# A transformer block's w_down in seven products: the sums of its weights from accumulating DMAs, and another order of the products

## The chip, the core and the metric

The kernel runs on one core of a Trainium2 chip. The metric is the device time of one execution in microseconds, as the median of several executions. The engines of the core work side by side, each through its own queue in program order: TensorE (PE, with its weight loads as PEld), VectorE (DVE), ScalarE (ACT), GpSimd (POOL) and SyncE (SP), which here issues nearly all DMAs.

## What is computed

One block of a decoder on 512 tokens of width 1024, in float32: two token mixers, then an MLP, then a gated per-layer embedding. The change touches the MLP and the passage to the last part:

```python
h2 = rms_norm(x, norm_mlp[i])
x = x + jnp.square(jax.nn.relu(h2 @ w_up[i])) @ w_down[i]        # 1024 -> 4096 -> 1024

ple_gate = jax.nn.sigmoid(rms_norm(x, norm_ple[i]) @ w_ple_gate[i])
x = x + ple_gate * (p[i] @ w_ple[i])
```

## The kernel before

Every float32 product is made of three matmuls (`mm3`, lines 100 to 104): an operand is split into an upper half (an ACT copy, rounded) and a lower half (DVE, the difference; `halves`, lines 161 to 164), and upper times upper, upper times lower and lower times upper are added up in PSUM. So each weight tile of 512 KB that comes in by DMA costs a 128x1024 copy on ACT and a 128x1024 subtraction on DVE. The halves rotate through three buffers each (`whi`, `wlo`), so that a tile can be split once the tile three before it is used up. The raw tiles have three buffers too (`raw`).

The order of the work is written out by hand. A *tick* is a point in the program after each half block, 12 matmuls of 128x128 by 128x512; a block (one output tile of w_up, or one product below) is two half blocks. `at(t, f)` puts work on tick t, and `spawn` starts a generator that goes on by a step at each tick (a `yield n` waits n ticks); what is emitted at a tick stands on each engine's queue at that place. Engines and DMA queues are bound to the order within their own queue and by the semaphores of the data, not to ticks as such.

The MLP starts at tick T0 = 178 and goes through the hidden layer in four quarters of 1024 hidden units, 30 ticks each. A quarter has eight tiles of w_up (U0 to U7; `unit` loads each seven ticks ahead of its use and `make` starts its split three ticks ahead), whose ReLU-squared outputs stand in `F`. Then w_down's quarter is multiplied by seven products in place of eight, after Strassen and Winograd: with activations A and weights split in two by two parts (A11, A12, A21, A22 below are the weights' parts, two tiles each), products are made of sums of parts, and their results are added to `acc` in several places. The diff names them P1 to P7; they run as P5, P1, P6, P2, P7, P3, P4, and U0 to U3 of the next quarter are put between the last four (`up_ahead`).

Two kinds of sums are needed. The weights' sums are made by GpSimd (`add`, line 282, eight for each quarter): A21 + A22 for P5, plus A11 for P6, plus A12 for P3, in a slot v; A21 + A11 for P7. The activations' sums (lines 879 to 888): each tile of U0 to U3 gives its part of the difference for P5, on GpSimd; each of U4 to U7 changes the first half of F in place, on GpSimd for U4 to U6 and on DVE for U7, one tick after its square. From these the operands are split into `ta` and `tb` (`later`, lines 910 to 917): P5 and P1 use ta, P6 and P2 use tb, P7 and P3 ta again, P4 tb. P6 reads the finished sum of the first half, P2 the second half as it came out of w_up, P1 the first half as it was before U4.

After the last quarter, `turn_back` transposes `acc` by TensorE back to the layout of x, adds it to x1 (which came back from DRAM as `x2`), splits the result scaled by the norm's gain, and adds up its squares; two of its four calls stand within and behind the last product, P4, at the ticks TP - 2 and TP - 1 (TP = T0 + 120 is where the embedding starts), the other two between the first matmuls of w_ple. The last call spawns `norm_end`, which sums over the partitions by a matmul (lines 364 and 365) and leads to R2. `load_p` loads the embedding's input p and splits it.

Of the kernel before, what the change touches and what calls it, by code (L numbers as in the profile page):

```python
# [21 lines left out]
F32 = mybir.dt.float32  # L22
# [24 lines left out]
def kernel(ctx: ExitStack, tc: tile.TileContext, xT, pT, w_in, w_val, w_glr, w2, cols,  # L47
# [213 lines left out]
    def make(raw):  # L261
# [2 lines left out]
        ready.append((hi, lo))  # L264
        jobs.insert(0, [halves(hi, lo, raw), 0])

    def down_units(g):

        d0 = T0 + 30 * g + 16
        gap = 2 if g < 3 else 0  # L270
        box = {}

        def load(t, name, tag, src):
            def f():
                if name not in box:
                    box[name] = [slot(f"{tag[0]}{int(tag[1:]) + j}", [P, 2, 512]) for j in range(2)] \
                        if tag[0] == "v" else slot(tag, [P, 2, 2, 512])
                nc.sync.dma_start(out=box[name][:, t % 2], in_=src)
            return f

        def add(out, a, b):
            G.tensor_tensor(out(), a(), b(), ALU.add)  # L282

        for u in range(2):
            a11, a12 = w_down[0, 4 * g + u], w_down[0, 4 * g + 2 + u]
            a21, a22 = w_down[1, 4 * g + u], w_down[1, 4 * g + 2 + u]

            def W(name, u=u):
                return lambda: box[name][:, u]

            def S(u=u):
                if u not in sums:
                    sums[u] = slot(f"v{u}", [P, 2, 512])
                return sums[u]
# [11 lines left out]
            at(d0 + u + 3, lambda W=W: make(W("A12")()))  # L306
            at(d0 + u + 4, load(u, "A22b", "c1", a22))
            at(d0 + u + 4, lambda S=S, W=W: add(S, S, W("A12")))
            at(d0 + u + gap + 5, lambda W=W: make(W("A21")()))
            at(d0 + u + 2 * gap + 7, lambda S=S: make(S()))  # L310
            at(d0 + u + 3 * gap + 9, lambda W=W: make(W("A22b")()))

    sums = {}
    for g in range(4):
        for j in range(8):
            c = T0 + 30 * g + 2 * j
            unit(c if g == 0 or j > 3 else c - 6 + 2 * j, w_up[8 * g + j, 0])
        at(T0 + 30 * g + 8, sums.clear)
        down_units(g)
    TP = T0 + 120  # L320
    unit(TP, w_ple[0])
    for j in range(8):
        unit(TP + 2 + 2 * j, w_gate[j, 0])
# [532 lines left out]
    def half_of(t):  # L856
        return t.rearrange("p (t c) -> p t c", t=2)

    ffs = {}

    def ahead_of(g):

        F = slot("a0", [P, 2, KT, 256])
        box = []

        def up_evac(i, ps):
            e = F[:, :, i]
# [5 lines left out]
            def rest():  # L873
                if not g and not i:
                    yield 2
                    V.tensor_tensor(e, e, half_of(R1), ALU.mult)
                A.activation(e, e, AF.Square)  # L877
                yield 1
                k = i % 4
                if i < 4:  # L880
                    if not box:
                        box.append(slot("c2", [P, 4, 256]))
                    G.tensor_tensor(box[0][:, k], F[:, 0, i], F[:, 1, i], ALU.subtract)  # L883
# [5 lines left out]
            spawn(rest())  # L889

        ffs[g] = F, up_evac, box
        return up_evac

    ahead_of(0)

    def up_down(g):
        nonlocal acc
        u0 = T0 + 30 * g
        d0 = u0 + 16
        F, up_evac, box = ffs.pop(g)  # L900
        ta = slot("a1", [P, 2, 2, 4, 256], F32R)
        tb = slot("a2", [P, 2, 2, 4, 256], F32R)

        def t_split(t, i, src):
            yield from halves(t[:, i, 0], t[:, i, 1], src)

        def later(t, gen):
            at(t, lambda: spawn(gen))
# [5 lines left out]
        later(d0 + 4, t_split(ta, 0, F[:, 1, :4]))  # L914
        at(d0 + 4, lambda: G.tensor_tensor(F[:, 0, 4:], F[:, 0, 4:], F[:, 0, :4], ALU.subtract))
        later(d0 + 6, t_split(ta, 1, F[:, 1, 4:]))
        later(d0 + 8, t_split(tb, 0, F[:, 0, 4:]))

        gemm_fm(8 if g == 0 else 4, kt_of(h2_hi, h2_lo), lambda i, ps: up_evac(i + (4 if g else 0), ps))

        if acc is None:
            acc = slot("a6", [P, NT, D])

        def part(n, t, m):
            return acc[:, 2 * t + m, n * T:(n + 1) * T]

        def product(t, i):
            ps = [bank(), bank()]
            for u in range(2):
                w = ready.pop(0)  # L930
                for k in range(2):
                    for m in range(2):
                        ms = slice(m * P, (m + 1) * P)
                        mm3(ps[m], (t[:, i, 0, 2 * u + k, ms], t[:, i, 1, 2 * u + k, ms]),
                            (w[0][:, k], w[1][:, k]), u == 0 and k == 0, u == 1 and k == 1)
                if u == 0:
                    tick()
            return ps

        new = g == 0  # L940
        ahead = ahead_of(g + 1) if g < 3 else None

        def up_ahead(i):
            if ahead:
                gemm_fm(1, kt_of(h2_hi, h2_lo), lambda _, ps: ahead(i, ps))

        for m, ps in enumerate(product(ta, 0)):
            subtotal(new, part(0, 1, m), ps, ALU.add)
            subtotal(new, part(1, 1, m), ps, ALU.subtract)
        tick()  # L950
        y = [tt("y"), tt("y")]
        for m, ps in enumerate(product(ta, 1)):
            A.activation(y[m], ps, AF.Copy)
            subtotal(new, part(0, 0, m), ps, ALU.add)
        tick()
        for m, ps in enumerate(product(tb, 0)):
            V.tensor_tensor(y[m], ps, y[m], ALU.subtract)
            G.tensor_tensor(part(0, 1, m), part(0, 1, m), y[m], ALU.subtract)
        tick()
        for m, ps in enumerate(product(tb, 1)):  # L960
            subtotal(False, part(0, 0, m), ps, ALU.add)
        tick()
        up_ahead(0)
        for m, ps in enumerate(product(ta, 0)):
            V.tensor_tensor(y[m], ps, y[m], ALU.add)
            G.tensor_tensor(part(1, 1, m), part(1, 1, m), y[m], ALU.add)
            if new:
                G.tensor_scalar(part(1, 0, m), y[m], 1.0, 1.0, ALU.mult, ALU.mult)
            else:
                G.tensor_tensor(part(1, 0, m), part(1, 0, m), y[m], ALU.add)  # L970
        tick()
        up_ahead(1)
        for m, ps in enumerate(product(ta, 1)):
            subtotal(False, part(0, 1, m), ps, ALU.add)
        tick()
        if g == 3:
            at(d0 + 12, lambda: turn_back(0))
            at(d0 + 13, lambda: turn_back(2))
        up_ahead(2)
        for m, ps in enumerate(product(tb, 0)):  # L980
            subtotal(False, part(1, 0, m), ps, ALU.add)
        tick()
        up_ahead(3)

    def turn_back(i0):

        nonlocal s2, R2
        for i in range(i0, i0 + 2):
# [34 lines left out]
    for g in range(4):  # L1023
        up_down(g)


    mid = slot("a1", [P, KT, T])
# [132 lines left out]
```

## Time and profile before

| | us |
|---|---|
| median of 3 runs | 1000.03 |
| lowest and highest | 999.83, 1000.47 |
| the profiled execution | 999.96 |
| its span, from the first to the last instruction | 998.2 |
| around the span | 1.8 |

| engine | busy us | share of the span |
|---|---|---|
| PE (matmul) | 965.1 | 97% |
| PEld (weight load, beside PE) | 799.5 | 80% |
| DVE | 634.9 | 64% |
| ACT | 471.0 | 47% |
| POOL (GpSimd) | 302.9 | 30% |

The MLP lies between about 565 and 918 us of the span. Times in the rows are microseconds from the span's start, unless marked ns. A timeline row gives start, duration, engine, line, operation and the tiles written and read, with the idle time in front of it and who ended it in brackets. A matmul's duration is longer than its distance from the next one, since matmuls overlap; their pace is read from the starts. PEclk is the granted clock of TensorE as a share of full speed, so that 1.00 is 2.4 GHz and 0.50 is 1.2 GHz.

### The profile page before, as it was taken

To read this page: it belongs to the slowest core of one execution; us is meant where nothing else is said; L and a number is where in the kernel's file an instruction comes from. 1 tells how busy PE (TensorE), PEld (TensorE's weight loads), DVE (VectorE), ACT (ScalarE), POOL (GpSimd) and SP (SyncE) were. 2 spreads that over 40 slices of the span, in tenths; PEclk is the share of its full clock that TensorE was granted. 3 is DMA by queue.
4 is the path that set the end of the run, shared out by engine and by line. 5 is a ranking of instruction groups with operands and counts; after the bars stand their busy time and mean duration, and the time that the engine had idled before them with its cause. 6 is when DMAs were issued, how large, how long until landed. Compare 5 with 4: busy or idle time off the path is not lost.

```text
span 998.2 us, 11425 instructions
## 1 busy us (share of the span) xinstructions
PE 965.1 (97%) x4360; PEld 799.5 (80%) x4360; DVE 634.9 (64%) x807; ACT 471.0 (47%) x691; POOL 302.9 (30%) x200
## 2 busy tenths in 40 slices
PE   9999999999999999999999998999899999989698
PEld 7888888878888888888888887888688778867586
DVE  5468889785456843333555557755874776589564
ACT  5558879773237632122323445423533433344551
POOL 0027656411220000000000038427652934665300
PEclk9999999999999999999999999999899989989799
DMA  7222111113211223343233443115214311551041
GB/s 254 85 84 85 64 57 64 64 64 106 85 61 45 88 103 105 106 169 106 85 105 127 148 169 133 57 59 193 85 64 169 122 68 43 190 190 42 22 148 42
DMA packets 29430, 101.22 MB, mean 101 GB/s; under 512 B 3392, under 2 KB 3776, under 8 KB 28992
## 3 DMA queue, kind: packets, MB, share of 16 engines
q1 hardware_dynamic: 29232, 100.48, 28.7%
q8 instruction: 34, 0.56, 0.2%
q14 instruction: 20, 0.16, 0.1%
q10 hardware_dynamic: 144, 0.02, 0.0%
HBM read 96.29 MB, written 4.19 MB: 101 GB/s over the span
## 4 chain that ended last, share of the span: by engine, by line
PE 88%; DVE 8%; ACT 2%; issue 1%; POOLq 0%; POOL 0%; ACTq 0%; DVEq 0%
PE acc L102 22%; PE acc L103 22%; PE acc L104 22%; PE aux L104 6%; PE aux L103 6%; PE aux L102 6%; DVE wlo L164 3%; DVE a L164 2%; DVE a L850 1%; PE aux L562 1%; ACT whi L162 1%; PE aux L729 1%; PE aux L365 1%; PE aux L364 1%; PE aux L732 1%
## 5 line engine op out<-in xcount | busy, mean ns | idle before, releaser
L102 PE MATMUL acc<-a,whi 128*128 128x512 f32 x832 | 326.4, 392 | 0.0
L103 PE MATMUL acc<-a,whi 128*128 128x512 f32 x832 | 324.3, 390 | 0.0
L104 PE MATMUL acc<-a,wlo 128*128 128x512 f32 x832 | 324.1, 390 | 0.0
L164 DVE TENSOR_TENSOR wlo<-raw,whi 128x1024 fp32r<-128x1024 f32 x128 | 167.7, 1313 | 79.3 <-ACT whi L162 77.9
L104 PEld LDWEIGHTS acc<-a,wlo 128*128 128x128 f32 x832 | 156.3, 188 | 32.9
L102 PEld LDWEIGHTS acc<-a,whi 128*128 128x128 f32 x832 | 156.6, 188 | 32.2
L103 PEld LDWEIGHTS acc<-a,whi 128*128 128x128 f32 x832 | 156.5, 188 | 31.8
L162 ACT ACTIVATE whi<-raw 128x1024 fp32r<-128x1024 f32 x128 | 134.2, 1049 | 86.6 <-PE acc L103 73.3
L104 PE MATMUL aux<-whi,a 128*128 128x512 f32 x288 | 116.9, 406 | 14.9 <-DVE a L164 14.9
L883 POOL TENSOR_TENSOR c<-a 128x256 f32<-128x256 f32 x16 | 13.8, 863 | 340.3 <-ACT a L877 340.3
L102 PE MATMUL aux<-whi,a 128*128 128x512 f32 x288 | 116.8, 406 | 0.0
L103 PE MATMUL aux<-wlo,a 128*128 128x512 f32 x288 | 115.9, 402 | 0.0
L104 PEld LDWEIGHTS aux<-whi,a 128*128 128x128 f32 x288 | 56.6, 197 | 28.6 <-DVE a L164 16.6
L164 DVE TENSOR_TENSOR wlo<-c,whi 128x1024 fp32r<-128x1024 f32 x32 | 53.0, 1672 | 22.9 <-ACT whi L162 22.9
L102 PEld LDWEIGHTS aux<-whi,a 128*128 128x128 f32 x288 | 56.7, 197 | 12.7 <-ACT a L162 0.8
L103 PEld LDWEIGHTS aux<-wlo,a 128*128 128x128 f32 x288 | 56.7, 197 | 12.5 <-DVE wlo L164 0.4
L162 ACT ACTIVATE whi<-c 128x1024 fp32r<-128x1024 f32 x32 | 33.9, 1060 | 60.7 <-PE aux L104 39.7
L877 ACT ACTIVATE a<-a 128x512 f32<-128x512 f32 x32 | 20.0, 627 | 68.2 <-DVE a L869 64.8
L492 POOL TENSOR_TENSOR ql<-q,qh 128x512 fp32r<-128x512 f32 x16 | 22.3, 1392 | 87.1 <-ACT qh L490 87.1
L282 POOL TENSOR_TENSOR v<-v,c 128x1024 f32<-128x1024 f32 x16 | 45.8, 2861 | 8.3 <-DVE wlo L164 8.3
L164 DVE TENSOR_TENSOR a<-a,a 128x1024 fp32r<-128x1024 f32 x24 | 43.3, 1804 | 6.6 <-ACT a L162 6.6
L164 DVE TENSOR_TENSOR wlo<-v,whi 128x1024 fp32r<-128x1024 f32 x24 | 41.2, 1742 | 7.6 <-ACT whi L162 7.6
(211 smaller groups left out, 1387.7 us busy)
## 6 DMA issues: line engine op xcount, KB each, us to landing
raw<-in_w_in_dram SPq DMA_DIRECT2D x48, 512.0 KB, 3.2
c<-in_w_down_dram SPq DMA_DIRECT2D x40, 512.0 KB, 5.5
raw<-in_w_up_dram SPq DMA_DIRECT2D x32, 512.0 KB, 3.4
raw<-in_w_val_dram SPq DMA_DIRECT2D x14, 512.0 KB, 3.3
raw<-in_w_a_dram SPq DMA_DIRECT2D x8, 512.0 KB, 3.3
raw<-in_w_b_dram SPq DMA_DIRECT2D x8, 512.0 KB, 3.3
raw<-in_w_out_dram SPq DMA_DIRECT2D x8, 512.0 KB, 3.3
raw<-in_w_gate_dram SPq DMA_DIRECT2D x8, 512.0 KB, 3.3
```

What stands on the lines that cost most here:

```text
L102: PE.matmul(ps, a[0], b[0], start=start, stop=False)
L103: PE.matmul(ps, a[0], b[1], start=False, stop=False)
L104: PE.matmul(ps, a[1], b[0], start=False, stop=stop)
L162: A.activation(hi, src, AF.Copy)
L164: (eng or V).tensor_tensor(lo, src, f32(hi), ALU.subtract)
L282: G.tensor_tensor(out(), a(), b(), ALU.add)
L364: PE.matmul(ps, ones[n], sh, start=True, stop=False)
L365: PE.matmul(ps, ones[n], sl, start=False, stop=True)
L492: G.tensor_tensor(sl, q2, f32(sh), ALU.subtract)
L562: PE.transpose(ps[:, c + (i - b) * P:c + (i - b + 1) * P], p[:, i, b * P:(b + 1) * P], ident)
L877: A.activation(e, e, AF.Square)
L883: G.tensor_tensor(box[0][:, k], F[:, 0, i], F[:, 1, i], ALU.subtract)
```

## The change

The weights' sums are no longer added by GpSimd from two tiles in SBUF. The first part is loaded into the sum's tile, and each further part is added to it by a DMA that GpSimd issues with `accum_op=ALU.add`, which reads the part from DRAM and adds it to what stands in the tile. In the last quarter the sum for P3 is made anew in two raw tiles by a load and three such DMAs each (`last_sum`), rather than carried on from P6's.

The order of the blocks becomes U4 U5 U6 P5 U7 P1 P2 P6 U0' P7 U1' P3 U2' P4 U3' in each quarter (the primes are the next quarter's tiles), so that P5 stands ahead of U7, and P2 ahead of P6. The loads, sums and splits take their ticks from the blocks' starts. For U7, square, differences and the split for P2 are emitted together in its evacuation; the other tiles keep their tick between the square and the differences. `norm_end` of x2 starts a tick later, and the load and the split of p move towards TP: the load from tick TP - 11 to TP - 4, the split from about TP - 5 to TP - 3.

```diff
+    blocks = [("U", 0, j) for j in range(4)]
+    for g in range(4):
+        mix = ["U4", "U5", "U6", "P5", "U7", "P1", "P2", "P6", "n0", "P7", "n1", "P3", "n2", "P4", "n3"]
+        for z in mix:
+            k = int(z[1])
+            if z[0] != "n":
+                blocks.append((z[0], g, k))
+            elif g < 3:
+                blocks.append(("U", g + 1, k))
+    start = {z: T0 + 2 * j for j, z in enumerate(blocks)}
+    TP = T0 + 2 * len(blocks)
+
     def down_units(g):
...
+        c = {k: start["P", g, k] for k in range(1, 8)}
...
-        def add(out, a, b):
-            G.tensor_tensor(out(), a(), b(), ALU.add)
...
+        def add(t, name, u, src):
+            at(t, lambda: G.dma_start(out=of(name, u), in_=src, accum_op=ALU.add))
+
+        def use(k, name, u):
+            at(c[k] + u - 3, lambda: make(of(name, u)))
...
-            at(d0 + u - 8, load(u, "A21", "c0", a21))
-            at(d0 + u - 8, load(u, "A22", "c3", a22))
-            at(d0 + u - 5, load(u, "A11", "c1", a11))
-            at(d0 + u - 5, lambda S=S, W=W: add(S, W("A21"), W("A22")))
-            at(d0 + u - 3, lambda S=S: make(S()))
-            at(d0 + u - 1, lambda S=S, W=W: add(S, S, W("A11")))
-            at(d0 + u - 1, lambda W=W: make(W("A11")()))
-            at(d0 + u - 1, load(u, "A12", "c3", a12))
-            at(d0 + u + 1, lambda S=S: make(S()))
-            at(d0 + u + 2, lambda W=W: add(W("A21"), W("A21"), W("A11")))
...
-            at(d0 + u + 4, lambda S=S, W=W: add(S, S, W("A12")))
...
+            t = c[5] + u
+            S = f"S{u}"
+            load(t - 10, S, f"v{u}", u, a22)
+            load(t - 9, "A21", "c0", u, a21)
+            load(t - 8, "A11", "c1", u, a11)
+            load(t - 1, "A12", "c3", u, a12)
+            load(c[1] + u, "A22", "c1", u, a22)
+            add(t - 8, S, u, a21)
+            add(t - 5, "A21", u, a11)
+            add(t - 1, S, u, a11)
+            if g < 3:
+                add(c[6] + u - 1, S, u, a12)
+            else:
+                last_sum(t, u, (a22, a21, a11, a12))
+            for k, name in ((5, S), (1, "A11"), (6, S), (2, "A12"), (7, "A21"), (3, S), (4, "A22")):
+                if g < 3 or k != 3:
+                    use(k, name, u)
+                else:
+                    at(c[3] + u - 3, lambda u=u: make(sums[u]))
...
+    def last_sum(t, u, srcs):
+
+        def f():
+            sums[u] = wp.tile([P, 2, 512], F32, tag="raw", name=nm("raw"))
+            nc.sync.dma_start(out=sums[u], in_=srcs[0])
+        at(start["U", 3, 7] + u - 6, f)
+        for j in range(3):
+            at(start["U", 3, 7] + u + 3 * j - 4, lambda j=j: G.dma_start(out=sums[u], in_=srcs[j + 1],
+                                                                     accum_op=ALU.add))
...
+    def quarter(g):
...
+        e7 = start["U", g, 7] + 1
...
+        c5 = start["P", g, 5]
+        at(c5 - 6, begin)
+        later(c5 - 4, lambda: t_split(ta, 0, t1))
+        later(c5 - 5, lambda: t_split(ta, 1, F[:, 0, :4]))
+        later(e7 + 1, lambda: t_split(tb, 0, F[:, 0, :4]))
+        later(e7 + 3, lambda: t_split(ta, 0, F[:, 1, :4]))
+        at(e7 + 4, t4_sum)
+        later(e7 + 5, lambda: t_split(ta, 1, F[:, 1, 4:]))
+        later(start["P", g, 6] + 2, lambda: t_split(tb, 0, F[:, 0, 4:]))
...
-        later(d0 - 6, t_split(ta, 1, F[:, 0, :4]))
-        at(d0 - 5, lambda: spawn(t_split(ta, 0, box[0])))
-        later(d0 + 2, t_split(tb, 0, F[:, 0, :4]))
-        later(d0 + 3, t_split(tb, 1, F[:, 0, 4:]))
...
-                yield 1
+                if i < 7:
+                    yield 1
+                pieces()
...
+            if i < 7:
+                spawn(squares())
+            else:
+                for _ in squares():
+                    pass
+                for _ in t_split(tb, 1, F[:, 0, 4:]):
+                    pass
...
-                spawn(norm_end(R2, s2))
+                spawn(norm_end(R2, s2), 1)
...
-        yield 6
+        yield 1
         p_hl = slot("c0", [P, 4, T], F32R)
...
-    at(T0 + 106 + 1, back_x1)
-    at(T0 + 106 + 3, lambda: spawn(load_p()))
+    at(start["P", 3, 1] + 1, back_x1)
+    at(start["P", 3, 3], lambda: spawn(load_p()))
+    at(TP - 2, lambda: turn_back(0))
+    at(TP - 1, lambda: turn_back(2))
```

## Rows read from the trace of the kernel before

**Rows 1.** the page's first part: busy us (share) xinstructions

```profile
PE 965.1 (97%) x4360; PEld 799.5 (80%) x4360; DVE 634.9 (64%) x807; ACT 471.0 (47%) x691; POOL 302.9 (30%) x200
```

**Rows 2.** who TensorE waited for, whole span: total us, times, longest

```profile
PE aux L104 <- DVE a L164: 14.9, 4, 3.7
PE acc L102 <- ACT a L1052: 6.3, 2, 3.7
...
PE aux L991 <- DVE a L850: 2.2, 2, 1.9
PE aux L364 <- ACT qh L92: 2.0, 1, 2.0
```

**Rows 3.** timeline, TensorE, first quarter: start us, us, instruction [idle]

```profile
609.11 0.39 PE L104 MATMUL acc<-a,wlo 128*128 128x512 f32 x1
609.33 0.39 PE L102 MATMUL aux<-whi,a 128*128 128x512 f32 x1
...
620.44 0.39 PE L103 MATMUL aux<-wlo,a 128*128 128x512 f32 x1
624.51 0.67 PE L104 MATMUL aux<-whi,a 128*128 128x512 f32 x1 [3.69 <-DVE a L164]
...
628.26 0.39 PE L104 MATMUL aux<-whi,a 128*128 128x512 f32 x1
```

**Rows 4.** stretches: length, PE, PEld, DVE, ACT, POOL busy (x), PEclk, DMA

```profile
620.43:628.25 7.82, 4.13 (x11) 2.97 (x10) 6.30 (x4) 3.40 (x6) 4.32 (x2) 0.78 0.57 225
707.39:717.01 9.62, 5.89 (x15) 4.34 (x15) 7.89 (x7) 3.29 (x5) 4.84 (x2) 0.65 0.49 195
795.46:805.62 10.16, 6.43 (x16) 4.76 (x16) 7.89 (x6) 3.83 (x6) 5.39 (x2) 0.66 0.46 179
883.85:894.41 10.56, 6.82 (x17) 5.09 (x17) 8.21 (x8) 4.23 (x6) 5.64 (x2) 0.68 0.45 178
712.46:716.30 3.84, 3.84 (x10) 2.97 (x9) 2.83 (x3) 0.00 (x0) 0.87 (x1) 0.50 0.02 9
```

**Rows 5.** timeline, DVE, same stretch

```profile
610.45 2.09 DVE L164 TENSOR_TENSOR wlo<-c,whi 128x1024 fp32r<-128x1024 f32 x1 [2.76 <-ACT whi L162]
612.46 0.68 DVE L869 SCALAR_TENSOR_TENSOR a<-acc,R 128x512 f32<-128x512 f32 x1
...
617.01 1.43 DVE L887 TENSOR_TENSOR a<-a 128x256 f32<-128x256 f32 x1
618.48 0.42 DVE L888 TENSOR_TENSOR a<-a 128x256 f32<-128x256 f32 x1
...
621.09 3.37 DVE L164 TENSOR_TENSOR a<-a,a 128x1024 fp32r<-128x1024 f32 x1
...
625.52 1.21 DVE L164 TENSOR_TENSOR a<-a,a 128x1024 fp32r<-128x1024 f32 x1
```

**Rows 6.** timeline, ACT, then GpSimd (POOL), same stretch

```profile
609.36 1.06 ACT L162 ACTIVATE whi<-c 128x1024 fp32r<-128x1024 f32 x1 [3.82 <-issue]
...
613.27 0.61 ACT L877 ACTIVATE a<-a 128x512 f32<-128x512 f32 x1
...
620.12 3.26 POOL L282 TENSOR_TENSOR v<-v,c 128x1024 f32<-128x1024 f32 x1 [1.96 <-DVE wlo L164]
```

**Rows 7.** the page's costliest groups: one of three forms of line 282

```profile
L282 POOL TENSOR_TENSOR v<-v,c 128x1024 f32<-128x1024 f32 x16 | 45.8, 2861 | 8.3 <-DVE wlo L164 8.3
```

**Rows 8.** all loads of w_down: ns to issue, then us to landing

```profile
L278 SPq DMA_DIRECT2D c<-in_w_down_dram x40: 327/426/479, 584.2 to 882.2; - x40
...
DMA to landing us min/median/max: 3.3/5.5/9.7
```

**Rows 9.** DMA issues: count, KB each, median us to landing

```profile
a<-spill SPq DMA_DIRECT2D x1, 2048.0 KB, 7.5
```

**Rows 10.** timeline, DVE, the end of the last quarter

```profile
912.70 2.32 DVE L164 TENSOR_TENSOR c<-raw,c 128x1024 fp32r<-128x1024 f32 x1
...
917.17 1.27 DVE L850 TENSOR_TENSOR a<-a,aux 128x512 f32<-128x512 f32 x2
```

More of the change, by code (lines that the diff above doesn't have):

```diff
@@ L314 @@
     for g in range(4):
         for j in range(8):
-            c = T0 + 30 * g + 2 * j
-            unit(c if g == 0 or j > 3 else c - 6 + 2 * j, w_up[8 * g + j, 0])
-        at(T0 + 30 * g + 8, sums.clear)
+            unit(start["U", g, j], w_up[8 * g + j, 0])
         down_units(g)
-    TP = T0 + 120
     unit(TP, w_ple[0])
@@ L857, in half_of, with t_split, begin, later @@
         return t.rearrange("p (t c) -> p t c", t=2)
-    ffs = {}
-    def ahead_of(g):
+    def t_split(t, i, src):
+        yield from halves(t[:, i, 0], t[:, i, 1], src)
+    def quarter(g):
         F = slot("a0", [P, 2, KT, 256])
-        box = []
+        ta = tb = t1 = y = None
+        e7 = start["U", g, 7] + 1
+        new = g == 0
+        def begin():
+            nonlocal acc, ta, tb
+            if new:
+                acc = slot("a6", [P, NT, D])
+            ta = slot("a1", [P, 2, 2, 4, 256], F32R)
+            tb = slot("a2", [P, 2, 2, 4, 256], F32R)
+        def later(t, f):
+            at(t, lambda: spawn(f()))
+        def t4_sum():
+            G.tensor_tensor(F[:, 0, 4:], F[:, 0, 4:], F[:, 0, :4], ALU.subtract)
+        c5 = start["P", g, 5]
[7 more added lines that the diff above has]
+        later(start["P", g, 6] + 2, lambda: t_split(tb, 0, F[:, 0, 4:]))
         def up_evac(i, ps):
+            nonlocal t1
             e = F[:, :, i]
@@ L937, in product @@
                     tick()
[L938 to L968, printed above, removed]
-            else:
-                G.tensor_tensor(part(1, 0, m), part(1, 0, m), y[m], ALU.add)
@@ L971, in up_down, with block @@
[L971 to L983, printed above, removed]
+            return enumerate(ps)
+        def block(z, i):
+            nonlocal y
+            if z == "U":
+                gemm_fm(1, kt_of(h2_hi, h2_lo), lambda _, ps: up_evac(i, ps))
+                return
+            if i == 5:
+                for m, ps in product(ta, 0):
+                    subtotal(new, part(0, 1, m), ps, ALU.add)
+                    subtotal(new, part(1, 1, m), ps, ALU.subtract)
+            elif i == 1:
+                y = [tt("y"), tt("y")]
+                for m, ps in product(ta, 1):
+                    A.activation(y[m], ps, AF.Copy)
+                    subtotal(new, part(0, 0, m), ps, ALU.add)
+            elif i == 6:
+                for m, ps in product(tb, 0):
+                    V.tensor_tensor(y[m], ps, y[m], ALU.subtract)
+                    G.tensor_tensor(part(0, 1, m), part(0, 1, m), y[m], ALU.subtract)
+            elif i == 2:
+                for m, ps in product(tb, 1):
+                    subtotal(False, part(0, 0, m), ps, ALU.add)
+            elif i == 7:
+                for m, ps in product(ta, 0):
+                    V.tensor_tensor(y[m], ps, y[m], ALU.add)
+                    G.tensor_tensor(part(1, 1, m), part(1, 1, m), y[m], ALU.add)
+                    if new:
+                        G.tensor_scalar(part(1, 0, m), y[m], 1.0, 1.0, ALU.mult, ALU.mult)
+                    else:
+                        G.tensor_tensor(part(1, 0, m), part(1, 0, m), y[m], ALU.add)
+            elif i == 3:
+                for m, ps in product(ta, 1):
+                    subtotal(False, part(0, 1, m), ps, ALU.add)
+            else:
+                for m, ps in product(tb, 0):
+                    subtotal(False, part(1, 0, m), ps, ALU.add)
+            tick()
@@ L985, in turn_back @@
+        return block
     def turn_back(i0):
@@ L1016, in load_p @@
         nc.sync.dma_start(out=raw, in_=pT)
-        yield 6
+        yield 1
         p_hl = slot("c0", [P, 4, T], F32R)
         yield from halves(p_hl[:, :2], p_hl[:, 2:], raw)
-    at(T0 + 106 + 1, back_x1)
-    at(T0 + 106 + 3, lambda: spawn(load_p()))
-    for g in range(4):
-        up_down(g)
+    at(start["P", 3, 1] + 1, back_x1)
+    at(start["P", 3, 3], lambda: spawn(load_p()))
+    at(TP - 2, lambda: turn_back(0))
+    at(TP - 1, lambda: turn_back(2))
+    quarters = {}
+    for z, g, i in blocks:
+        if g not in quarters:
+            quarters[g] = quarter(g)
+        quarters[g](z, i)
     mid = slot("a1", [P, KT, T])
```

56 lines of the change are left out of this document (12 added, 44 removed).

## The prediction

> **What bounds the kernel now.** TensorE is busy 965.1 of the span's 998.2 us [rows 1], so a change can win only where TensorE stands still or runs slowly. The next view is who TensorE waits for [rows 2]: 14.9 us of waiting, the largest entry, goes to DVE line 164 in four waits of at most 3.7 us. There is one such wait in each quarter of the MLP, always in front of the third matmul of P6, the third product; the first is the gap from 620.44 to 624.51 [rows 3]. After each of them the matmuls are slow for a while: the granted clock is 0.50, the 1.2 GHz level, over 712.46 to 716.30 [rows 4].
>
> What one wait costs. At the full clock 49 matmuls lie between the first matmul of P5 at 609.33 and the one at 620.44 [rows 3]: 11.11/49 = 0.2267 us each, 2.72 us for a half block of 12 and 5.44 us for a block of 24. Each of the first four stretches of [rows 4] reaches from the last matmul ahead of the gap (one more for the last three) to the first at full pace again. Its count less one, times 0.2267, is what it should take: 7.82 - 10 x 0.2267 = 5.55; 9.62 - 14 x 0.2267 = 6.45; 10.16 - 15 x 0.2267 = 6.76; 10.56 - 16 x 0.2267 = 6.93. Together **25.7 us**: 14.9 waited, 10.8 through the lower clock.
>
> Why DVE is late. P6 needs a split of sums that exist only after w_up's last tile U7. In the first quarter U7's last matmul starts at 609.11 [rows 3]. ACT then makes a weight's upper half at 609.36 [rows 6]. DVE takes 2.09 us for the lower half, the ReLU stands behind it at 612.46, the subtraction of line 887 ends at 618.44, and the split for P6 takes 3.37 us from 621.09, to 624.46 [rows 5]. That is 15.1 us after U7's end (about 609.3); its cover, P5 and P1, lasts 10.9. Two things stretch the chain: a wait of one tick and other work in between, and GpSimd. The same 128x1024 subtraction takes 1.21 us at 625.52 and 3.37 us at 621.09 [rows 5], where GpSimd adds quarters of w_down from 620.12 on for 3.26 us [rows 6].
>
> **The change part by part.** I write half blocks (2.72 us) from the start of a quarter's P5 = 0; the new order puts U7 at +2, P1 at +4, P2 at +6, P6 at +8. The matmuls stay the same, so TensorE's own work is unchanged.
>
> 1. *P6 moves behind P2.* U7's end to P6 is now P1 and P2, 10.9 us as before, but the split for P6 is spawned at +4, with no quarter sums on GpSimd beside it. Its old wait of 3.7 us goes, with the clock that it cost: **-25.7 us**.
>
> 2. *P2 comes to stand where the wait could reappear.* It follows U7 after P1 alone, 5.44 us. Its own split is now made directly in U7's evacuation, without a tick. The chain, with durations from [rows 5, 6]: ACT upper half at +0.25 after U7's last start, DVE lower half 1.22 (1.21 undisturbed) from +1.34 to +2.56, ReLU 0.68 to +3.2, square 0.6 to +3.9, the two subtractions at 0.42 to +4.85, with ACT's half of the split beside them (about 1.05, from +3.85 to +4.9), DVE's half 1.22 to +6.2. P2's third matmul, the first that reads that lower half, falls due 27 matmuls after U7's last, at 27 x 0.2267 = +6.12. So a wait of 0.1 us; bounds 0 and 0.5 a quarter. **+0.5 us** for four.
>
> 3. *GpSimd's 32 adds become accumulating DMAs, 36 issues of 512 KB.* One of the 16 adds into v takes 2.86 us [rows 7]. What an issue occupies GpSimd for is not in this trace: at least SP's 0.43 us for the same transfer [rows 8], at most about the 2.9 of the add that it replaces. I take the upper end, since even so 36 x 2.9 = 104 us is spread over some 350, and the subtractions queued behind an issue (U5's and U6's, due for the split at +4) still come in time. Nothing, 0.
>
> 4. *How long one takes to land* (D) is not in the trace either. A load of a w_down quarter lands in 3.3 to 9.7 us [rows 8]; a 2 MB load in 7.5 [rows 9]. An accumulation reads source and destination and writes once, at most 1.5 MB moved: between the two, 3.3 + (7.5 - 3.3) x 1/1.5 = 6.1 us is my estimate, 9 with an issue of 2.9 ahead. The tightest sum is P5's: A22 loaded at -10, A21 added on GpSimd's queue at -8 (in effect -7), its split (1.05 on ACT, 1.22 on DVE) needed by 0, so ready at -0.85: 6.1 half blocks, **16.7 us**. The others have as much or more, except P3's in the last quarter, three accumulations one after another from about -1 to +11: 12 half blocks, 33 us, 11 us each. Both lie above 9, so 0. GpSimd waits for each load's landing and for the splits that read the old sum; queued behind are the subtractions, with three half blocks of slack. SP's queue gets 42 loads for 40, most at earlier ticks, and nothing there waits for a slot that is still in use at its tick.
>
> 5. *The tail.* p's load and split move from about eleven and five half blocks ahead of TP to four and three. In the trace p's lower split (2.32 us from 912.70) stands ahead of P3's subtotals at 917.17 on DVE [rows 10], and the transposes wait 2.2 us for these [rows 2]. After the change it stands behind them, but still ahead of turn_back's first add, so DVE, which sets the tail from there on (L1052's 6.3 us [rows 2]), reaches that add at about the same time: 0, bounds -2 and +2. The norm of x2 starts one tick later: its matmul (line 364) waits 2.0 us now [rows 2]. It moves behind 12 more matmuls, 2.72 us, while its input is pushed back behind about 1 us of ACT work. I count **-1.5**, bounds -2.5 and 0.
>
> Sum: 999.96 (profiled execution: span 998.2 and 1.8 around it; the median of the runs is 1000.03, the same) - 25.7 + 0.5 - 1.5 = 973.3; I say **973.5**.
>
> **The rivals.**
>
> *The wait moves to P2.* For it: item 2 has no margin. If DVE is still slowed, as by GpSimd in [rows 5] (2.09 for 1.21, and 2.4 instead of 1.2 for the split, about 1 more in the subtraction), P2 waits 3.1 us, plus some 2.7 at the low clock: 4 x 5.8 = 23, total 996. At half of that, 985. Against it: nothing is put on GpSimd's queue between U7's end and P2 in the first three quarters but what was late. Chance 0.14, more on the lower half.
>
> *The accumulations are late, and it is slower.* Place: the split of P5's first sum on ACT, behind which everything of ACT stands. It decides from D = 16.7 us on; each us beyond is one us per quarter, with some 2.7 for the clock. To lose the 25 us of the other items, 6.3 a quarter, D has to reach about 20 us; at D = 25 it is 4 x (8.3 + 2.7) = 44 against 26.7, total 1018. For it: the slowest plain load took 9.7 us [rows 8], and twice that, 19.4, would be 2.7 beyond: 4 x (2.7 + 2.7) = 22 us lost, 995. Against it: the median is 5.5, with other loads in flight. The Trainium skill, "Collectives: The Full Stack", section "The bandwidth ceiling: the fold count and why AG ≠ RS ≠ AR", says that a reduction in the DMA path is slower because it reads two sources, at about half the rate of a copy; no run shows that here. By that rule the 19.4 us is the slowest landing to be met and 11.0 the median, so I give this case more than the rows of plain loads alone would. Chance of slower 0.09; of D between, with 985 to 998, 0.05.
>
> *It does not do what it says.* Issuing on GpSimd could hold it and DVE as long as the adds did, and the split for P6 would be late again behind P2: about 1000, as before. Against it: an issue reads no two operands through the port that the rows show contended, and P6's split starts earlier. Chance 0.04.
>
> *More than forecast*: the tail's waits on DVE shrink as well, 966 to 970: 0.04.
>
> **How the numbers follow.** Forecast (970 to 977) 0.64, P2 0.14, late accumulations 0.05 and 0.09, nothing gained 0.04, more 0.04. The range runs from 969 to 988: the forecast with its bounds, most of the P2 case, the upper edge of the last one; about 0.2 is left out, nearly all above. Faster by over 0.2% (a change of 2 us, about what a measurement of this kernel can tell from none): 0.64 + 0.14 + 0.05 + 0.04, 0.87; within 0.2%: 0.04; slower: 0.09.
>
> **What would show it.** Right: no wait for DVE line 164 of over 0.5 us in any quarter, 30 half blocks in 81.6 us each, the clock at 1.00 through the MLP, the weights' lower halves near 1.22 us. Item 2 is wrong if P2's third matmul waits over 1 us; items 3 and 4 if ACT waits for a DMA into v ahead of P5 or P3, or GpSimd's subtractions come late for P6; item 5 if line 364 still waits 2 us, or the transposes start late. The forecast falls altogether if an accumulation takes over 17 us.

## The result, and the profile after

| | before | changed kernel |
|---|---|---|
| median time, us | 1000.25 (999.83 to 1000.94) | **977.04** (976.64 to 977.64) |
| ratio, 95% interval | | 0.9768 [0.9751, 0.9785] |
| profiled execution: time, span, us | 999.96, 998.2 | 977.64, 975.9 |
| granted clock, whole span | 0.980 | 0.993 |

Faster by 23.2 us. The forecast was 973.5 in a range of 969 to 988: the time lies in the range, 3.5 us above the forecast and at the upper edge of the 970 to 977 that was given most of the chance.

The page of the changed kernel, its first two parts (busy us, share, instructions; then the granted clock in 40 slices):

```profile
span 975.9 us, 11466 instructions
PE 956.2 (98%) x4360; PEld 791.7 (81%) x4360; DVE 619.1 (63%) x807; ACT 470.1 (48%) x691; POOL 232.3 (24%) x204
...
PEclk9999999999999999999999999999999999999799
```

Against [rows 1], TensorE has the same 4360 matmuls and is busy 8.9 us less, since nearly all of them now run at the full clock. GpSimd is busy 70.6 us less. The span is 22.3 us shorter.

Who TensorE waits for in the changed kernel, whole span (us in total, times, longest):

```profile
PE acc L102 <- ACT a L1078: 7.1, 2, 4.5
PE aux L359 <- DVE ones L355: 2.2, 1, 2.2
PE aux L1012 <- DVE a L871: 1.7, 3, 1.1
PE acc L104 <- DVE wlo L164: 1.6, 3, 0.6
PE aux L103 <- DVE wlo L164: 1.5, 2, 0.9
```

The 14.9 us at the head of [rows 2], the waits for P6's split, are gone. So is the wait of the norm's matmul (line 364, now 385). The transposes (line 991, now 1012) wait 1.7 for 2.2. New are five short waits, 3.1 us, for `wlo`, a weight's lower half.

Where the time came from is read in one stretch of each kernel, from 600.00 to the first transpose behind the MLP. Windows of the kernel before and then of the changed one (length, busy us and counts of PE, PEld, DVE, ACT, POOL, granted clock, DMA share, GB/s):

```profile
600.00:915.58 315.58, 300.69 (x1278) 245.84 (x1278) 226.37 (x198) 131.60 (x147) 176.40 (x92) 0.96 0.30 109
```

```profile
600.00:895.35 295.35, 292.27 (x1279) 239.16 (x1279) 206.19 (x197) 129.64 (x146) 104.62 (x92) 1.00 0.63 176
```

The counts of matmuls agree to one, so the stretches hold the same work. At 0.2267 us a matmul [rows 3], 1278 of them should take 289.7 us: before lost 315.58 - 289.7 = **25.9 us** here. The changed kernel lost 295.35 - 1279 x 0.2267 = **5.4 us**. I call this figure the MLP's loss and use it for every run below; it is good to about 0.5 us, since a matmul at an edge or a missing record moves it by 0.2. The rest, span less first transpose, is the tail: 998.2 - 915.6 = 82.6 before, 975.9 - 895.4 = 80.5 now. So 25.9 - 5.4 = 20.5 us came from the MLP and 2.1 from the tail, where 25.2 and 1.5 were forecast. What is missing, some 4.7 us, is in the MLP.

### The profile page after: what moved, and what is told of

It is laid out like the page before. It is cut to its first block, busy times and chain, and to the rows that moved or that the text cites. A ratio compares the mean times of both kernels' runs of the same rounds, so it can differ in the third digit from the quotient of the medians.

```text
span 975.9 us, 11466 instructions
## 1 busy us (share of the span) xinstructions
PE 956.2 (98%) x4360; PEld 791.7 (81%) x4360; DVE 619.1 (63%) x807; ACT 470.1 (48%) x691; POOL 232.3 (24%) x204
## 3 DMA queue, kind: packets, MB, share of 16 engines
q0 software_dynamic: 5184, 18.88, 10.1%
## 4 chain that ended last, share of the span: by engine, by line
PE 85%; DVE 9%; ACT 3%; issue 2%; POOL 0%; DVEq 0%; ACTq 0%; POOLq 0%
PE acc L102 22%; PE acc L104 22%; PE acc L103 22%; PE aux L103 5%; PE aux L104 5%; PE aux L102 5%; DVE wlo L164 3%; DVE a L164 2%; DVE a L871 1%; ACT whi L162 1%; PE aux L583 1%; PE aux L750 1%; PE aux L386 1%; PE aux L385 1%; PE aux L753 1%
## 5 line engine op out<-in xcount | busy, mean ns | idle before, releaser
L164 DVE TENSOR_TENSOR wlo<-raw,whi 128x1024 fp32r<-128x1024 f32 x130 | 172.7, 1331 | 95.8 <-ACT whi L162 94.6
L162 ACT ACTIVATE whi<-raw 128x1024 fp32r<-128x1024 f32 x130 | 136.4, 1050 | 108.1 <-PE acc L103 71.3
L103 PE MATMUL aux<-wlo,a 128*128 128x512 f32 x288 | 112.3, 390 | 1.5 <-DVE wlo L164 1.5
L104 PE MATMUL aux<-whi,a 128*128 128x512 f32 x288 | 112.6, 391 | 0.0
L102 PE MATMUL aux<-whi,a 128*128 128x512 f32 x288 | 112.2, 390 | 0.0
L103 PEld LDWEIGHTS aux<-wlo,a 128*128 128x128 f32 x288 | 54.1, 188 | 13.6 <-DVE wlo L164 2.4
L104 PEld LDWEIGHTS aux<-whi,a 128*128 128x128 f32 x288 | 54.1, 188 | 12.6 <-DVE a L164 1.5
L102 PEld LDWEIGHTS aux<-whi,a 128*128 128x128 f32 x288 | 54.1, 188 | 11.1
L925 ACT ACTIVATE a<-a 128x512 f32<-128x512 f32 x32 | 20.1, 630 | 71.9 <-DVE a L917 68.6
L164 DVE TENSOR_TENSOR wlo<-c,whi 128x1024 fp32r<-128x1024 f32 x32 | 48.8, 1555 | 8.7 <-ACT whi L162 8.7
L162 ACT ACTIVATE whi<-c 128x1024 fp32r<-128x1024 f32 x32 | 33.7, 1055 | 31.4 <-PE acc L103 12.4
L102 PE MATMUL acc<-c,whi 128*128 128x512 f32 (+1 forms) x82 | 32.9, 402 | 7.2 <-ACT a L1078 7.1
L810 ACT ACTIVATE a<-a 128x512 f32<-128x512 f32 x16 | 10.1, 632 | 61.5 <-DVE a L809 61.5
L871 DVE TENSOR_TENSOR a<-a,aux 128x512 f32<-128x512 f32 x42 | 27.1, 681 | 17.0 <-PE aux L104 17.0
## 6 DMA issues: line engine op xcount, KB each, us to landing
c<-in_w_down_dram SPq DMA_DIRECT2D x32, 512.0 KB, 10.1
```

The lines of the kernel that those rows point to most:

```text
L102: PE.matmul(ps, a[0], b[0], start=start, stop=False)
L103: PE.matmul(ps, a[0], b[1], start=False, stop=False)
L104: PE.matmul(ps, a[1], b[0], start=False, stop=stop)
L162: A.activation(hi, src, AF.Copy)
L164: (eng or V).tensor_tensor(lo, src, f32(hi), ALU.subtract)
L810: A.activation(s, s, AF.Sigmoid)
```

## The experiments

The theory after the result: the weights' sums on GpSimd made DVE late in the kernel before; the new order's part is to leave room for accumulations that land late; and the 5.4 us that are still lost come from one large GpSimd operation that stayed, line 901. The rivals: the order did it alone; the accumulations cost the rest; the loads of the last quarter are late. All times are medians with the kernel before run beside them.

**1. The new order, with the sums on GpSimd.** Each accumulation becomes a plain load of its own and an add by GpSimd:

```
+                    G.tensor_tensor(of(out, u), of(p, u), of(q, u), ALU.add)
...
+            load(t - 9, "A22x", "c3", u, a22)
...
+            sum_up(t - 5, S, "A21", "A22x")
...
-            add(t - 8, S, u, a21)
```

`sum_up` puts the first of these lines on a tick. The other sums are made likewise, that for P3 in the last quarter by one more add to P6's.

> The changed kernel with its new order of the blocks, but the weights' sums added by GpSimd from tiles in SBUF as before. If the order alone brings the gain: P6's wait stays away, P2 waits 0 to 1 us, 976 to 982 us. If the gain hangs on taking the sums off GpSimd (the additions slow DVE's subtractions from 1.22 to 2.1 to 3.4 us, and two of them, A21 + A11, run on GpSimd around U7's end): P2's third matmul waits 2 to 3 us in each quarter with some 2.5 us of low clock behind it, 990 to 1000 us.

992.67 us, ratio 0.9927 [0.9912, 0.9942]. The time is in the range of the second expectation, but no wait is as long as the 2 to 3 us that it named, and the granted clock is 1.00 over the whole MLP. The waits have not gone, they have spread; who TensorE waited for:

```profile
PE aux L103 <- DVE wlo L164: 6.2, 7, 1.5
PE acc L104 <- DVE wlo L164: 3.9, 3, 1.4
PE aux L102 <- ACT a L162: 2.7, 4, 0.7
...
PE aux L104 <- DVE a L164: 2.1, 4, 0.5
```

The cause in the timeline, GpSimd's adds and DVE's splits in the same stretch (start, us; a row of x3 is three instructions):

```profile
697.15 5.73 POOL L313 TENSOR_TENSOR c<-c,c 128x1024 f32<-128x1024 f32 x2
697.41 7.69 DVE L164 TENSOR_TENSOR wlo<-c,whi 128x1024 fp32r<-128x1024 f32 x3
```

Three splits took 7.69 us, where three undisturbed ones take 3 x 1.21 [rows 5]. The MLP's loss is 310.64 - 1276 x 0.2267 = 21.4 us: the order alone brings 4.5 of the 20.5.

**2. The old order, without the four adds of each quarter and half.** The weights' sums are left out of the computation; the operands that are split are single parts (A22 and A21) instead.

```
-            at(d0 + u - 8, load(u, "A22", "c3", a22))
+            at(d0 + u - 8, lambda S=S, a22=a22: nc.sync.dma_start(out=S(), in_=a22))
-            at(d0 + u - 5, lambda S=S, W=W: add(S, W("A21"), W("A22")))
-            at(d0 + u - 1, lambda S=S, W=W: add(S, S, W("A11")))
-            at(d0 + u + 2, lambda W=W: add(W("A21"), W("A21"), W("A11")))
-            at(d0 + u + 4, lambda S=S, W=W: add(S, S, W("A12")))
```

> The kernel before in its old order, with the additions of w_down's parts left out (A22 stands in for the three sums in v, A21 for A21 + A11), so that GpSimd doesn't add beside DVE and no accumulating DMA runs. If DVE's slowing beside GpSimd was the cause of P6's wait: the chain from U7 to P6's split shrinks from 15.1 by some 5.3 us (2.09 and 2.50 to 1.22, 1.43 to 0.42, 3.37 to 1.22) to 9.8 us, under its cover of 10.9, the four waits vanish and the time is 974 to 977 us. If the order was the cause (the tick between the square and the differences, the splits that stand ahead): P6 still waits 1.5 us or more in each quarter, 988 to 996 us.

980.44 us, 0.9799 [0.9784, 0.9814]. P6 still stands where it stood, and its wait has all but gone; the time is some 4 us above the 974 to 977 expected:

```profile
PE aux L104 <- DVE a L164: 1.8, 4, 0.4
```

From 14.9 [rows 2] to 1.8, with the order untouched. The loss is 294.48 - 1277 x 0.2267 = 5.0; the tail is 82.6, as before.

**3. The old order, with accumulating DMAs** at the ticks of the old adds, but for A21 + A11, which moves six half blocks ahead:

```
-            G.tensor_tensor(out(), a(), b(), ALU.add)
+            G.dma_start(out=out(), in_=src, accum_op=ALU.add)
...
-            at(d0 + u + 2, lambda W=W: add(W("A21"), W("A21"), W("A11")))
+            at(d0 + u - 4, lambda W=W, a11=a11: add(W("A21"), a11))
```

> The kernel before in its old order, with the weights' sums made by accumulating DMAs at the ticks of the old additions (A21 + A11 earlier, as soon as A21 is there). If taking the sums off GpSimd is what counts and the accumulations (9 to 12 us to land, 0.87 us to issue) fit in the old order as well: 977 to 984 us. If the new order is what makes room for them: P6's sum has some 10.5 us between P5's splits and its own, ACT waits for it with the splits for P6 and P2 queued behind, and P6's third matmul or its weights come 2 us or more late in each quarter: 986 to 998 us.

987.12 us, 0.9875 [0.9858, 0.9891]; loss 301.95 - 1280 x 0.2267 = 11.8. ACT waits for the sums, and TensorE with it, longest in the last quarter (2.62 us at 873.33); from ACT's waits and its timeline:

```profile
ACT whi L162 <- DMA v<-in_w_down_dram: 39.3, 12, 5.9
```

```profile
871.27 1.06 ACT L162 ACTIVATE whi<-v 128x1024 fp32r<-128x1024 f32 x1 [4.86 <-DMA v<-in_w_down_dram]
```

ACT's longest wait of all, 5.9 us, is for P5's sum, which by its ticks could have been started earlier in the old order too; that wasn't tried. So this is the price of the accumulations at these ticks.

**4. The new order, the first accumulation five half blocks later.**

```
-            add(t - 8, S, u, a21)
+            add(t - 3, S, u, a21)
```

> The changed kernel with P5's accumulation (A21 onto A22) put on GpSimd's queue three ticks ahead of P5 instead of eight, so that it lies behind the differences of the tiles ahead. Theory (the prediction's limit for the landing time): the second one is issued about 7.4 us ahead of P5, lands 10.6 us later, and its split ends some 3 us after the second half of P5 falls due; with the low clock behind it some 5.5 us per quarter: about 999 us, between 990 and 1005. Rival: the accumulation lands much faster when nothing else is in flight, or ACT's queue has room: 977 to 982 us.

990.38 us, 0.9906 [0.9891, 0.9921]; loss 308.45 - 1281 x 0.2267 = 18.1. The same wait on ACT, and behind it TensorE's:

```profile
ACT whi L162 <- DMA v<-in_w_down_dram: 41.2, 8, 7.7
```

```profile
PE aux L103 <- DVE wlo L164: 4.7, 6, 1.3
...
PE aux L102 <- ACT whi L162: 4.1, 3, 3.5
```

The direction was right, the size smaller (990 for 999 expected). The prediction's second rival is thus a real mechanism of this kernel; the change keeps clear of it by the place of its first accumulation.

**5. No accumulations at all.** All 36 are left out of the computation (`add` as below, and the loop of `last_sum`); the plain loads stay.

```
-            at(t, lambda: G.dma_start(out=of(name, u), in_=src, accum_op=ALU.add))
+            pass
```

> The changed kernel with all 36 accumulating DMAs left out (each sum is its first part alone), the plain loads kept: what the accumulations cost now. If they lie beside other work throughout: 976 to 977.5 us, no change, although the plain loads land in about 5 us again instead of 10. If their traffic or GpSimd's issuing costs time (the waits for weights in the last quarter): 972 to 975 us.

978.12 us, 0.9781 [0.9766, 0.9795]: the same as with them; loss 295.94 - 1279 x 0.2267 = 6.0. By itself that doesn't show that they cost nothing, since the two losses are made up differently. In the changed kernel GpSimd comes to P4's difference (line 901, here 898) only behind an accumulation that waits for DVE, at 709.30; here it comes to it at 703.31, beside another split of DVE's, and TensorE waits 1.30 us in three of the quarters. GpSimd's timeline and TensorE's:

```profile
703.31 3.25 POOL L898 TENSOR_TENSOR a<-a 128x1024 f32<-128x1024 f32 x1 [11.75 <-DVE a L164]
```

```profile
710.03 0.50 PE L103 MATMUL aux<-wlo,a 128*128 128x512 f32 x1 [1.30 <-DVE wlo L164]
```

What bounds the accumulations' cost is run 6, which keeps all 36 and loses 1.4 us in all. They do load the DMA engines: without them the loads of w_down into `c` land in 6.6 us, with them in 10.1 (median).

**6. P4's difference on DVE instead of GpSimd.**

```
         def t4_sum():
-            G.tensor_tensor(F[:, 0, 4:], F[:, 0, 4:], F[:, 0, :4], ALU.subtract)
+            V.tensor_tensor(F[:, 0, 4:], F[:, 0, 4:], F[:, 0, :4], ALU.subtract)
```

> The changed kernel with the one difference for P4 (128x1024, line 901) on DVE instead of GpSimd. Theory: on GpSimd it blocks DVE's subtraction beside it (3.65 and 3.90 us for 1.22), and so the lower half of the next tile's weight comes 0.45 to 0.94 us late in every quarter. On DVE it costs 1.22 us and blocks nothing, and these waits go: about 3.3 us less, 973 to 975 us. Rival: DVE is late there by its own amount of work, the extra 1.22 us makes the waits longer: 977 to 980 us.

**972.81 us**, 0.9729 [0.9714, 0.9743]; loss 290.63 - 1276 x 0.2267 = 1.4. Of the `wlo` waits one of 0.3 us is left. DVE's timeline in the stretch that is shown for the changed kernel further down:

```profile
707.79 1.22 DVE L164 TENSOR_TENSOR a<-a,a 128x1024 fp32r<-128x1024 f32 x1
...
710.12 1.22 DVE L901 TENSOR_TENSOR a<-a 128x1024 f32<-128x1024 f32 x1
711.26 1.22 DVE L164 TENSOR_TENSOR wlo<-raw,whi 128x1024 fp32r<-128x1024 f32 x1
```

The subtraction costs DVE 1.22 us and gives it back about 2.4 on the split.

**7 to 9. The tail and the last sum.** One undoes the norm's extra tick, one p's later load and split; one leaves out the separate sum of the last quarter and carries its P3 sum on by one more accumulation.

```
-                spawn(norm_end(R2, s2), 1)
+                spawn(norm_end(R2, s2))
```

> The changed kernel with the last norm's sum started one tick earlier again, as before the change. Theory: the matmul of line 385 (364 before) waits 2.0 us again, with some 0.4 us of low clock: 979 to 980 us. Rival: the wait only changes places in the tail: 977 us, no change.

```
-         yield 1
+         yield 6
-    at(start["P", 3, 3], lambda: spawn(load_p()))
+    at(start["P", 3, 1] + 1, lambda: spawn(load_p()))
```

> The changed kernel with p's load and split back at their old ticks (load at TP - 11, split at about TP - 5). By the prediction's item 5: p's lower half stands ahead of P3's subtotals on DVE again and the transposes start some 2 us later, but turn_back's first addition comes at the same time: 976 to 978 us, no change. Rival: the later split is worth the wait of the transposes, 1.5 to 2 us: 978.5 to 979.5 us.

```
-            if g < 3:
-                add(c[6] + u - 1, S, u, a12)
-            else:
-                last_sum(t, u, (a22, a21, a11, a12))
+            add(c[6] + u - 1, S, u, a12)
```

> The changed kernel with P3's sum in the last quarter carried on from P6's by one more accumulation, as in the other quarters, instead of made anew in two raw tiles. There P3 follows P6 after P7 alone: between P6's splits and P3's own lie some 8 to 11 us, and an accumulation takes about 10.6 with its issue. Theory: P3's weights come 1 to 2.5 us late, once or twice, with some low clock: 979 to 983 us. Rival: fewer transfers in flight there (the tail's loads land sooner), nothing is late: 975.5 to 977.5 us.

The norm: 979.06 us, 0.9784 [0.9768, 0.9801]. The wait is back, and the tail grows from 80.5 to 979.3 - 895.1 = 84.2 us:

```profile
PE aux L385 <- ACT qh L92: 3.1, 1, 3.1
```

By the medians this is 2.0 us, by the tails 3.7 (the profiled execution is the slowest of its four, 980.98); the intervals of the two kernels overlap, so only that the wait returns is sure. p: 976.53, 0.9763 [0.9745, 0.978], tail 80.1: no difference. The last sum: 977.01, 0.977 [0.9752, 0.9787], and ACT's split has no wait for a DMA in front of it, so my expectation of 1 to 2.5 us fell. Its timeline:

```profile
882.86 1.06 ACT L162 ACTIVATE whi<-v 128x1024 fp32r<-128x1024 f32 x1 [2.64 <-PE aux L104]
```

`last_sum`, with its three accumulations one after another, isn't needed. In the changed kernel ACT does wait for them:

```profile
ACT whi L162 <- DMA raw<-in_w_down_dram: 4.8, 2, 2.4
```

**10. A version that is faster than both.** Beside the edit of 6, the end of the MLP makes both residual adds of a pair of tiles on DVE ahead of the two splits that wait for ACT:

```
             V.tensor_tensor(x2[:, i], ps, x2[:, i], ALU.add)
+        for i in range(i0, i0 + 2):
             scaled_split(h3[0][:, i], h3[1][:, i], x2[:, i], col[:, C_PLE + i:C_PLE + i + 1])
```

> The changed kernel with P4's difference on DVE, and in turn_back the two additions of a pair of tiles ahead of the two splits, so that DVE doesn't wait for ACT within each tile. Theory: what is left is bounded by the chain DVE, ACT, DVE of turn_back, 2.15 us a tile; in pairs it is about 1.45 to 1.6, some 4 to 5 us less for eight tiles, and TensorE's waits for the copies of line 1078 (7.1 us) shrink by as much: 966 to 969.5 us. Rival: the tail is held by the weights' halves on DVE: 971 to 973 us, as with P4's difference alone.

**968.78 us**, 0.9691 [0.9677, 0.9705]: 31.3 us below the kernel before as it ran beside it (1000.07). The tail goes from 80.4 (run 6) to 966.8 - 891.1 = 75.7. DVE's timeline, run 6 and then this one (the bracket is the idle time ahead of the instruction):

```profile
896.16 0.75 DVE L98 SCALAR_TENSOR_TENSOR a<-a,col,a 128x512 fp32r<-128x512 f32 x1 [0.79 <-ACT a L97]
```

```profile
895.13 1.27 DVE L1018 TENSOR_TENSOR a<-aux,a 128x512 f32<-128x512 f32 x2
...
896.60 0.75 DVE L98 SCALAR_TENSOR_TENSOR a<-a,col,a 128x512 fp32r<-128x512 f32 x1 [0.20 <-ACT a L97]
```

The second add now fills the time in which DVE had waited for ACT. The largest wait that is left is TensorE's 5.6 us for ACT line 1079 (7.1 for line 1078 in the changed kernel); it wasn't attacked.

**The sums and the order together**, the MLP's loss and the median time, in us:

| | sums by GpSimd | by accumulating DMA | left out |
|---|---|---|---|
| order of before | 25.9, 1000.25 | 11.8, 987.12 | 5.0, 980.44 |
| new order | 21.4, 992.67 | 5.4, 977.04 | 6.0, 978.12 |

Read along a row: leaving the adds out is worth 15 to 21 us of loss, making them by accumulating DMA 14 to 16. Read down: the order is worth 4.5 us with GpSimd's adds and 6.4 with accumulations, which at the ticks of run 3 land late for the old one. With nothing to add the two orders lose about the same, but the lower figure holds the price of line 901, which the new order brings (run 5); what the order is worth without that, no run shows. Neither half of the change alone reaches its time. (The times of the lower row also hold the tail's gain of some 2 us.)

## Why the prediction was right or wrong

**What bounds the kernel: right.** The four waits for P6's split, with the clock behind them, were what there was to gain. The runs sharpen the reason. Item 1 put the whole 25.7 us on P6's move; it named GpSimd's adds as what stretches the chain, and "with no quarter sums beside it" was half a sentence. Runs 1 and 2 show that this half sentence carries most of the gain and the move little by itself.

**The range: it held partly by luck.** Its room above the forecast was left for the bounds of items 2 and 5 and for a wait that moves to P2. These came out as forecast, and a term that the sum didn't contain took up the room.

**Item 2, P2's wait: right, to 0.1 us.** TensorE's timeline around P2's third matmul in the second quarter, and DVE's ahead of it:

```profile
703.50 0.39 PE L103 MATMUL aux<-wlo,a 128*128 128x512 f32 x1
703.85 0.50 PE L104 MATMUL aux<-whi,a 128*128 128x512 f32 x1
```

```profile
698.95 1.23 DVE L164 TENSOR_TENSOR wlo<-c,whi 128x1024 fp32r<-128x1024 f32 x1 [2.29 <-ACT whi L162]
700.09 0.68 DVE L917 SCALAR_TENSOR_TENSOR a<-acc,R 128x512 f32<-128x512 f32 x1
...
702.57 1.23 DVE L164 TENSOR_TENSOR a<-a,a 128x1024 fp32r<-128x1024 f32 x1 [0.21 <-ACT a L162]
```

0.35 from start to start for 0.2267: 0.12 us of wait, 0.1 forecast. The splits take 1.23, not 2.09 and 3.37 [rows 5]. The first rival, the wait moving to P2, didn't happen.

**What was missing: the operation that stayed on GpSimd.** The prediction followed DVE only from U7 to P2 and P6. Behind that, GpSimd makes P4's difference (line 901, line 915 before). GpSimd's timeline of the changed kernel, then DVE's, then TensorE's:

```profile
708.70 0.88 POOL L298 DMA_DIRECT2D v<-in_w_down_dram  x1 [16.50 <-DVE wlo L164]
709.30 2.70 POOL L901 TENSOR_TENSOR a<-a 128x1024 f32<-128x1024 f32 x1
791.91 2.70 POOL L901 TENSOR_TENSOR a<-a 128x1024 f32<-128x1024 f32 x1
...
877.07 2.73 POOL L901 TENSOR_TENSOR a<-a 128x1024 f32<-128x1024 f32 x1
```

```profile
709.45 3.65 DVE L164 TENSOR_TENSOR a<-a,a 128x1024 fp32r<-128x1024 f32 x1
...
714.22 1.21 DVE L164 TENSOR_TENSOR wlo<-raw,whi 128x1024 fp32r<-128x1024 f32 x1
...
876.99 3.90 DVE L164 TENSOR_TENSOR wlo<-c,whi 128x1024 fp32r<-128x1024 f32 x1
```

```profile
714.63 0.39 PE L103 MATMUL acc<-a,whi 128*128 128x512 f32 x1
715.48 0.50 PE L104 MATMUL acc<-a,wlo 128*128 128x512 f32 x1 [0.46 <-DVE wlo L164]
715.82 0.40 PE L102 MATMUL acc<-a,whi 128*128 128x512 f32 x1
...
880.95 0.50 PE L103 MATMUL aux<-wlo,a 128*128 128x512 f32 x1 [0.94 <-DVE wlo L164]
...
892.70 0.50 PE L103 MATMUL aux<-wlo,a 128*128 128x512 f32 x1 [0.58 <-DVE wlo L164]
```

A split of DVE starts 0.15 us behind the subtraction and takes 3.65 us for 1.22; DVE is 2.4 us behind from there on, and the next tile's weight comes late for its third matmul. So it goes in the first three quarters; in the last one it holds the split of P7's weight for 3.90 us. The row at 715.48 shows only 0.46 us of idle time, but the starts around it lie 0.85 and 0.34 apart for 0.2267 each, so this wait costs 0.74; at that rate the 3.1 us of the five new waits make some 4.5 us, an estimate, of the 5.4 that are lost.

The fifth of them, 0.58 at 892.70, isn't line 901's. P4's weights are split there beside the adds to `acc` that are on GpSimd too, and run 6 keeps 0.27 of that wait. GpSimd, then DVE:

```profile
891.52 2.27 POOL L995 TENSOR_TENSOR a<-a,y 128x512 f32<-128x512 f32 x1
```

```profile
890.72 4.16 DVE L164 TENSOR_TENSOR wlo<-c,whi 128x1024 fp32r<-128x1024 f32 x2
```

In the kernel before, P4's difference ran while DVE stood idle, here in the first quarter, between the splits of 625.52 [rows 5] and 629.78:

```profile
626.88 2.39 POOL L915 TENSOR_TENSOR a<-a 128x1024 f32<-128x1024 f32 x1 [3.50 <-DVE a L164]
```

```profile
629.78 1.23 DVE L164 TENSOR_TENSOR wlo<-c,whi 128x1024 fp32r<-128x1024 f32 x1 [3.05 <-ACT whi L162]
```

The new order moves work beside it. Run 6 prices it: 977.04 - 972.81 = 4.2 us, which is the missing 4.7 of the MLP but for the accuracy of the readings. This is the term that the sum lacked: of the subtractions on GpSimd the prediction asked only whether they come in time, not what they do to DVE. With it the sum of 973.3 would have been 977.5.

The split ends at 713.10, 1.1 us after GpSimd's 712.00. The Trainium skill, "SBUF — State Buffer", section "Who interferes with whom", says that a DVE instruction with two inputs in SBUF contends with a GpSimd instruction that reads SBUF, and that the port pair which the two engines share is an exclusive lock. The trace agrees: the split behaves as one of 1.2 us begun when GpSimd was through. Which of the two came first can't be read from these rows: the split of 876.99 starts 0.08 us ahead of GpSimd's subtraction and is held all the same.

**Item 3, the issue: the size was off, without effect.** All accumulations of line 298 into `v`, issue in ns, and the landing of those of the whole line:

```profile
L298 POOL DMA_DIRECT2D v<-in_w_down_dram x22: 857/873/1197, 582.8 to 855.9; - x22
...
DMA to landing us min/median/max: 5.3/9.7/13.9
```

0.87 us of GpSimd (into `c` up to 1.22), where 2.9 was taken as the upper end. Run 6 keeps the issues and loses 1.4 us in all, so they cost little. But what an issue waits for, as at 708.70, sets when line 901 runs behind it.

**Item 4, the landing: under-estimated, and covered.** D is 9.7 us in the median (line 298), at most 13.9, for 6.1 estimated; the limit of 16.7 for P5 held, and so the 0. The 11 us for each of P3's in the last quarter didn't: they land in 10.7 us, at most 12.4, and ACT waits for them 2.4 us twice; run 9, without them, is no faster. P5's limit was nearer than the estimate let it seem: in the old order, with less room, the same accumulations cost 11.8 - 5.0 = 6.8 us (run 3), and five half blocks less room for the first one cost 990.38 - 977.04 = 13.3 (run 4). The rival's 0.14 for late landings was fair. The Trainium skill, "Collectives: The Full Stack", section "The bandwidth ceiling: the fold count and why AG ≠ RS ≠ AR", says of the reductions in collectives that they run at about half a copy's rate, since the add reads two sources. The trace agrees roughly: against the same loads without accumulations beside them (6.6, run 5), 9.0 to 12.4 by target (the page's DMA issues) is 1.4 to 1.9 times, though here the loads beside them have a part in it. The prediction's 11.0 by that rule was nearer to the measured median than the 6.1 worked out from bytes.

**Item 5, the tail: right, a little small.** 2.1 us gained for 1.5 forecast; p costs nothing (run 8), and the norm's tick is worth about the 2.0 us that it was to hide (run 7, with overlapping intervals).

**The rivals' price of a wait: too high for short ones.** They put about 2.7 us of low clock behind every wait, also behind those of 1 us. Runs 1, 3 and 4, windows that begin where a wait ends (granted clock third from the end):

```profile
634.79:640.00 5.21, 5.21 (x23) 4.24 (x23) 5.21 (x4) 0.29 (x2) 3.44 (x2) 1.00 0.31 101
```

```profile
874.78:880.00 5.22, 5.22 (x16) 4.14 (x17) 3.41 (x4) 2.39 (x4) 1.66 (x1) 0.67 0.72 213
```

```profile
864.38:872.00 7.62, 6.85 (x16) 5.19 (x17) 5.78 (x8) 4.05 (x5) 6.85 (x7) 0.55 0.67 120
```

The first follows a wait of 1.43 us and has 23 matmuls in 5.21 us, at 1.00, the 2.4 GHz level. The second follows waits of 2.62 and 0.72 us, and has 16 in 5.22 at 0.67, between the two levels. The third follows 3.54 us and a further wait inside it, and has 16 in 7.62 at 0.55, near the 1.2 GHz level. Run 1 lost its 21.4 us without the clock's help (1.00 over the whole MLP, with waits of up to 1.5). So in this kernel a rival that spreads short waits over the quarters has to be priced without the clock; for waits of 2.7 and 3.1 us, which the rivals also name, runs 3 and 4 show that a lower clock can follow.

**What would show it.** Of the signs named ahead, "no wait for DVE line 164 of over 0.5 us in any quarter" failed: there are waits of 0.6 and 0.9, and it pointed to the term that was missing. So did the 81.6 us for 30 half blocks: from line 901 at 709.30 to the next at 791.91 it is 82.61. ACT waits for no DMA into v, but ahead of P3 in the last quarter for those into the raw tiles (run 9).

## What to carry to other kernels

When work is taken off an engine that slows another one, list every large operation that stays on it, and see what the new order puts beside each: one subtraction of 2.7 us on GpSimd in each quarter cost this kernel 4.2 us in all, and 1.22 us of DVE each bought it back. A step that takes longer to arrive can replace a faster one that disturbs, if the order leaves the room; change the two together, and test the four combinations to see which carries the gain. A run that leaves work out can move other work: look at what its loss is made of before you compare it.

## What the runs showed of the hardware

- An accumulating DMA of 512 KB occupies GpSimd for 0.87 us and lands in 9.7 us (median; 5.3 to 13.9, with other loads in flight); the splits for P2 and P6 take 1.22 to 1.23 us with the sums made by it, where beside GpSimd's adds one took 2.09 and one 3.37 [rows 5].
- It slows the transfers beside it: loads of 512 KB into `c` land in 10.1 us with accumulations and in 6.6 without; the one load of 2 MB in 16.6 with them and in 9.8 without (run 5).
- Waits of TensorE of up to 1.5 us left the granted clock at 1.00 (run 1); waits of 2.6 us (run 3), 3.5 (run 4) and 3.7 (before, [rows 4]) were followed by matmuls at the lower level.
